# Head-pair sums moved from GpSimd to VectorE, T blocks loaded in place, results loaded among the last Strassen groups, LN begun later

## The chip, the cores and the metric

One NeuronCore of a Trainium2 chip. The metric is device microseconds of one execution of the whole layer; lower is better. The engines are called PE (TensorE; PEld are its weight loads), DVE (VectorE), ACT (ScalarE), POOL (GpSimd) and SP (SyncE, which issues nearly all transfers here).

## The reference

One layer of a hybrid backbone, in fp32: a modulated RMSNorm, one input projection to 56 column tiles of 128 beside q, k and v, three branches, and a gated merge.

```python
h, gate = modulate(x, c, ...)                    # 1024 tokens x 1024
z = h @ w_in                                     # 1024 x (11*512 + 3*1024)
kc, vc = na_kv(hc @ w_in[:, A_K:A_Z], ...)       # 256 context tokens
ya = neighbourhood_attention(q, k, v, kc, vc, rpb) * silu(z[A_Z:B_B])   # 8 heads of 64
yb = z[B_B:B_C] * dw_conv(z[B_C:B_V] * z[B_V:B_Z], w3) * silu(z[B_Z:C_GLU])
u  = dw_conv(a * sigmoid(g), w31) + b            # a, g: two 512-wide parts of z
yc = silu(layer_norm(u)) * silu(z[C_Z:GATES])
m  = ga * (ya @ w_out_a) + gb * (yb @ w_out_b) + gc * (yc @ w_out_c)    # ga, gb, gc: sigmoid of z[GATES:]
x  = x + gate * (m @ w_o)
```

## The kernel before, in words

Every fp32 product is made of three: each operand is split into a high part and the rest (`hi`, `lo`), and hi x hi, hi x lo and lo x hi are added in PSUM. The activations lie transposed: h is 16 tiles, `ha0` to `ha7` for the first 512 tokens and `hb0` to `hb7` for the others, each with its high part and its low part (128 x 2 x 512). `ACT` makes high parts by a cast, POOL or DVE the low ones by a subtraction (L90, L639).

Stages, in time: modulation and h (to about 100 us); four head pairs (`attend`, `qkv` of the next pair, `glu`), to about 540 us; a stage of Strassen groups, 565 to 943 us; three merges by `wout`, with the LN of the conformer branch among them, and the last projection by `wo`.

**Attention.** A head is 8 units. In a unit PE makes scores `sc` and `sl`, DVE finds their maximum and adds the bias (L544, L547; the bias comes from POOL), ACT takes exponentials, DVE adds sums, takes the reciprocal and scales (L551 to L554) in one of four buffers `pbuf`, PE transposes (`pp`, L564), ACT and DVE split the transposed blocks (`ph`, `plo`), PE multiplies with v (`py`), and DVE adds the halves into `ya` (L577; four times per head). PE needs something else to do in between: that is `glu` in the earlier pairs, and in the last one `plain(ZA + i)` and `plain(BZ + i)`, which make 16 halves (each 24 products into a bank `zaps`; `ps_m` has two banks) and evict them through a `flt` tile: sigmoid by ACT, product by DVE, store by SP.

**Sums of h.** `h_sums(j)` makes the four combinations of blocks of h that the Strassen stage multiplies with (T1 to T4) for k-block j: four sums of a high and a low part (`whole`, L598) and four differences (`less`, L603), each 128 x 512, and stores the results to `td` in DRAM. It runs on POOL, one j in each head pair. Its tiles come from `tmp`, a pool of six buffers that `flt` uses as well.

**T blocks.** Before the Strassen stage `load_t` loads `td` into `traw` tiles and splits them into T1 to T3; T4 goes into the place of `hb0` to `hb3`.

**Strassen stage.** Groups of products (banks `ga` to `ge`, `gd`) of `wz` with blocks of h and T1 to T4; among them the 31-tap convolution on DVE (`conv_step`, L690), and `a_result`, which multiplies attention by its gate on POOL and stores the split result. `last_two` are the last two groups. All results go to DRAM: `ysd` (ya, yb), `cvd` (convolution), `gd` (gates), `zcd`.

**Merges.** `merge(br, ys, beside)` goes over 8 blocks and two halves, 12 products `ops` each; POOL or DVE adds to `mt` (L980). `norm_steps` is the LN, cut into steps that `beside` calls: column sums (`col_sums`, PE), variances (L1041, POOL), `rstd` (diagonal tiles by DVE, PE product, L1051, L1052), then per half a DVE product, two ACT functions and two POOL products (L1064, L1066), and a split into `yc`.

**Order.** The program is written in this sequence, and a list scheduler with a timeline model of its own then sets each engine's row; `tc.issue_after(x)` holds what is inside it behind instruction x. Tiles of a pool are taken in the order of the text: a tile waits until the tile that had its buffer before is done with. Pools opened at a place that another pool had wait for that one.

Of the kernel before, what the change touches and what calls it, by code (L numbers as in the profile page):

```python
# [42 lines left out]
def tile_hybrid(ctx: ExitStack, tc, x, xT, cx, cond, crow, ng, w_ada, b_ada, wqkv, wz,  # L43
# [5 lines left out]
    hctx = ExitStack()  # L49
    hp_pool = hctx.enter_context(tc.tile_pool(name="hT", bufs=1))  # L50
# [79 lines left out]
    def qkv(hp, w=None, cts=None, first=(), psc=None, mid=None):  # L130
# [41 lines left out]
        def context():  # L172
            vc = [a1.tile([P, 2, P], F32R, tag=f"vc{h}", name="vc") for h in range(2)]
# [64 lines left out]
    A_t = cst.tile([P, KT, 2], F32, name="A_t")  # L238
    B_t = cst.tile([P, KT, 2], F32, name="B_t")
# [224 lines left out]
    with tc.tile_pool(name="at", bufs=1, reuse_waits="tile") as at, \  # L464
# [45 lines left out]
        def attend(hp):  # L510
            ya = at.tile([P, 16, 64], F32, tag="ya", name="ya", bufs=1)
            for h in range(2):
# [9 lines left out]
                for cb in range(4):  # L522
# [54 lines left out]
                    dve.tensor_tensor(out=ya[hs, :, cb * 16 : cb * 16 + 16],  # L577
# [16 lines left out]
        def h_sums(j):  # L594

            def whole(o, k):
                t = tmp("hsum")
                pool.tensor_tensor(out=t, in0=hlf[o][k][:, 0].bitcast(F32), in1=hlf[o][k][:, 1].bitcast(F32), op=ALU.add)  # L598
                return t

            def less(i, a, b):

                pool.tensor_tensor(out=b, in0=a, in1=b, op=ALU.subtract)  # L603
                nc.sync.dma_start(td[i][j], b)
# [9 lines left out]
        for hp in range(4):  # L614
# [12 lines left out]

    sctx = ExitStack()
# [34 lines left out]
    for i in (1, 0, 2):  # L663
        load_t(T[i], i)
    load_t(T4, 3)
# [99 lines left out]

    def last_two(cts, uses):
# [24 lines left out]
        for n in two:  # L791
# [4 lines left out]
            dve.tensor_tensor(out=x[n], in0=f, in1=x[n], op=ALU.add)  # L796
        s3 = [s_(n, raw[n][0], raw[n][2], ALU.subtract, "s3") for n in two]
# [7 lines left out]
        for n in two:  # L805
# [5 lines left out]
            uses[n][1](0, y[n])  # L811
        s4 = [s_(n, raw[n][1], s2[n], ALU.subtract, "s4") for n in two]
# [90 lines left out]

    for i in range(4):
        u = b_start(i)
        gate_pair()
        b_end(i, u)
    halves = [(i, b) for i in range(4) for b in range(2)]
    for i in range(5):
# [5 lines left out]
        for _ in range(1 + (i in (0, 2, 4))):  # L915
            a_result(*halves.pop(0))
# [7 lines left out]
    hctx.close()  # L924
# [277 lines left out]
```

## Time and profile before

| what | value |
|---|---|
| median of 3 runs | 1202.31 us (1201.91 to 1203.02) |
| profiled execution | 1200.33 us, span 1198.5 us |
| mean granted TensorE clock | 0.964 |
| PE busy | 1126.9 us (94%), 5566 matmuls |
| DVE busy | 850.8 us (71%) |
| POOL busy | 663.4 us (55%) |
| ACT busy | 560.8 us (47%) |
| moved by DMA | 167.87 MB, 139 GB/s of HBM |

A busy time is the time in which an engine had an instruction running; matmuls are pipelined, so PE at 100% of a stretch may still be slow where the granted clock (PEclk) is low. The span is the profiled program; the execution's own time is 1.83 us longer, and 2.0 us under the median. In rows of groups stand: line, engine, operation, output<-inputs, shapes and count, then busy us and mean ns, then idle us before them and what ended it.

### The profile page before, as it was taken

How to read it: one execution, taken by the hardware profiler on the slowest of the kernel's cores; microseconds unless marked ns; L12 is line 12 of the kernel's file. 1: busy time of each engine (PE TensorE's matmuls, PEld its weight loads, DVE VectorE, ACT ScalarE, POOL GpSimd, SP SyncE). 2: the span in 40 equal slices, each digit the busy share in tenths (PEclk: the TensorE clock that was granted, in tenths of full speed). 3: DMA queues.
4: the chain of work that ended last, by engine and by line, in shares of the span. 5: the costliest groups of instructions: out<-in, count | busy, mean ns of one | idle time of the engine just before them, and what ended most of it. 6: DMA issues, size and time to landing. Idle time of an engine off the chain costs nothing.

```text
span 1198.5 us, 16663 instructions
## 1 busy us (share of the span) xinstructions
PE 1126.9 (94%) x5566; PEld 961.0 (80%) x5566; DVE 850.8 (71%) x1495; ACT 560.8 (47%) x1167; POOL 663.4 (55%) x623
## 2 busy tenths in 40 slices
PE   5779699999999999998999999999999798999998
PEld 4678699899899788886788888887877476888887
DVE  7995768788877875657993897896993356679311
ACT  5575358557656688784333332324334335313110
POOL 6675845645745833310887677868888006851110
PEclk7789899999999999999899999999999798999999
DMA  9235242332322313117234434345653694662621
GB/s 354 106 136 180 72 126 84 104 108 85 111 64 77 118 63 121 56 42 236 93 102 142 124 105 149 101 154 173 190 192 132 242 406 153 205 241 88 237 80 53
DMA packets 88151, 167.87 MB, mean 140 GB/s; under 512 B 11008, under 2 KB 39424, under 8 KB 88064
## 3 DMA queue, kind: packets, MB, share of 16 engines
q1 hardware_dynamic: 83456, 164.70, 40.9%
q10 hardware_dynamic: 4608, 2.10, 0.6%
q8 instruction: 44, 0.72, 0.3%
q14 instruction: 43, 0.35, 0.1%
HBM read 120.62 MB, written 46.14 MB: 139 GB/s over the span
## 4 chain that ended last, share of the span: by engine, by line
PE 59%; DVE 17%; DMA 8%; POOL 7%; issue 4%; ACT 3%; SPq 1%; POOLq 0%; DVEq 0%; ACTq 0%
DVE cv L690 4%; PE ops L107 4%; PE ops L109 4%; PE ops L108 4%; PE pp L564 3%; PE zaps L108 3%; PE zaps L107 3%; PE zaps L109 3%; PE ps L109 3%; PE ps L107 3%; PE ps L108 3%; PE fin L109 2%; PE fin L107 2%; PE fin L108 2%; DMA wada<-in_w_ada 2%
## 5 line engine op out<-in xcount | busy, mean ns | idle before, releaser
L90 POOL TENSOR_TENSOR wl<-wr,wh 128x384 fp32r<-128x384 f32 (+2 forms) x93 | 89.6, 969 | 182.2 <-ACT wh L88 156.1
L690 DVE SCALAR_TENSOR_TENSOR cv<-upad,cf_t,cv 128x512 f32<-128x512 f32 x240 | 166.9, 747 | 0.2
L88 ACT CAST wh<-wr 128x384 fp32r<-128x384 f32 (+2 forms) x138 | 61.2, 456 | 113.5 <-DMA wr<-in_wout 46.9
L533 POOL TENSOR_TENSOR bias<-mka,vimg 128x288 f32<-128x288 bf16 (+1 forms) x64 | 59.5, 931 | 87.8 <-DVE mn L547 76.5
L639 POOL TENSOR_TENSOR wl<-s,wh 128x512 fp32r<-128x512 f32 x57 | 79.5, 1409 | 11.1 <-ACT wh L638 6.4
L638 ACT CAST wh<-s 128x512 fp32r<-128x512 f32 x76 | 46.1, 616 | 75.6 <-POOL s L642 64.1
L639 POOL TENSOR_TENSOR wl<-wr,wh 128x512 fp32r<-128x512 f32 x46 | 64.4, 1402 | 22.7 <-ACT wh L638 22.7
L569 DVE TENSOR_TENSOR plo<-pp,ph 128x512 fp32r<-128x512 f32 (+1 forms) x96 | 60.8, 640 | 8.5 <-ACT ph L567 8.0
L714 PE MATMUL ga<-ha,wh 128*128 128x512 f32 x152 | 60.6, 398 | 6.5 <-ACT wh L638 4.7
L564 PE MATMUL pp<-ident,pbuf 128*128 128x128 f32 x352 | 59.1, 273 | 1.6 <-DVE pbuf L553 1.3
L716 PE MATMUL ga<-ha,wl 128*128 128x512 f32 x152 | 60.3, 397 | 0.2 <-POOL wl L639 0.2
L715 PE MATMUL ga<-ha,wh 128*128 128x512 f32 x152 | 60.2, 396 | 0.0
L567 ACT CAST ph<-pp 128x512 fp32r<-128x512 f32 (+1 forms) x96 | 51.7, 547 | 16.8 <-PE pp L564 16.0
L549 ACT ACTIVATE pbuf<-sc,mn 128x256 f32<-128x256 f32 x64 | 30.4, 475 | 60.1 <-DVE mn L547 59.6
L1116 DVE SCALAR_TENSOR_TENSOR o<-fin,gate,xr 128x512 f32<-128x512 f32 x16 | 12.0, 751 | 59.7 <-PE fin L109 59.7
L551 DVE TENSOR_TENSOR mn<-mn 128x1 f32<-128x1 f32 x64 | 17.6, 275 | 47.0 <-ACT pbuf L550 46.7
L109 PE MATMUL fin<-mh,wl 128*128 128x512 f32 x128 | 49.8, 389 | 0.0
L108 PE MATMUL fin<-ml,wh 128*128 128x512 f32 x128 | 49.8, 389 | 0.0
L107 PE MATMUL fin<-mh,wh 128*128 128x512 f32 x128 | 49.7, 389 | 0.0
L564 PEld LDWEIGHTS pp<-ident,pbuf 128*128 128x128 f32 x352 | 42.7, 140 | 7.0 <-DVE pbuf L553 2.6
L90 DVE TENSOR_TENSOR wl<-wr,wh 128x384 fp32r<-128x384 f32 (+2 forms) x45 | 31.6, 705 | 13.9 <-ACT wh L88 13.9
L79 POOL TENSOR_TENSOR ssh<-ssh,half_neg 128x4 f32<-128x4 f32 (+1 forms) x40 | 39.4, 987 | 2.7
(382 smaller groups left out, 3970.3 us busy)
## 6 DMA issues: line engine op xcount, KB each, us to landing
wr<-in_wz SPq DMA_DIRECT2D x36, 512.0 KB, 3.9
gs<-gd SPq DMA_DIRECT2D x24, 512.0 KB, 5.2
wada<-in_w_ada SPq DMA_DIRECT2D x16, 512.0 KB, 8.7
wr<-in_wz SPq DMA_DIRECT2D x36, 192.0 KB, 2.5
cht<-chd SPq DMA_DIRECT2D x24, 256.0 KB, 3.1
gd<-gate SPq DMA_DIRECT2D x22, 256.0 KB, 3.1
vimg<-in_rpbs SPq DMA_DIRECT2D x16, 288.0 KB, 3.0
gd<-c SPq DMA_DIRECT2D x18, 256.0 KB, 3.1
```

The costliest lines, as they stand in the source:

```text
L88: act.copy(hi[:, :n], raw[:, :n])
L90: state["lo"] = lo_eng.tensor_tensor(out=lo[:, :n], in0=raw[:, :n], in1=hi[:, :n].bitcast(F32), op=ALU.subtract)
L107: pe.matmul(ps, ah, bh, start=i == 0, stop=False)
L108: pe.matmul(ps, ah, bl, start=False, stop=False)
L109: pe.matmul(ps, al, bh, start=False, stop=i == n - 1)
L564: pe.transpose(out=pp[:, c * 256 + hf * P : c * 256 + hf * P + P], in_=pts[hf][:, o : o + P], identity=ident)
L569: dve.tensor_tensor(out=plo[:, : m * 256], in0=pp[:, : m * 256], in1=ph[:, : m * 256].bitcast(F32), op=ALU.subtract)
L639: eng.tensor_tensor(out=lo, in0=src, in1=hi.bitcast(F32), op=ALU.subtract)
L690: dve.scalar_tensor_tensor(out=acc[b], in0=src, scalar=cf_t[:, i, j : j + 1], in1=acc[b], op0=ALU.mult, op1=ALU.add)
L714: pe.matmul(ps, wh, bh, start=first and j == 0, stop=False, skip_group_check=True)
L715: pe.matmul(ps, wh, bl, start=False, stop=False, skip_group_check=True)
L716: pe.matmul(ps, wl, bh, start=False, stop=last and j == 3, skip_group_check=True)
```

## The change

Five things change.

1. `h_sums` runs on DVE in place of POOL, and all four j stand in the last head pair, held behind the last `ya` addition of the third pair. In the text they still come ahead of `plain(ZA + i)`.
2. T1 to T3 get a pool of their own, `tp`, that stays open; `load_t` loads raw blocks straight into the low tile and splits in place. T2, T1, T3 are loaded ahead of the last two `plain` gates, T4 after the first `b_start`.
3. The pools of h and T stay open to the end. `mt`, `cv`, `ya`, `yb` take tiles of them, by a table `homes`, and `yb`, half of `ya` and `cv` are loaded inside `last_two`; the other loads are where a tile becomes free.
4. `a_result` is called once in the first loop's later steps and once per step of the second loop.
5. The LN's steps begin in the third block of the first merge, three per half; `rstd` is made by two products of 512 columns in place of eight of 128, with empty steps between its parts.

```diff
-    hctx = ExitStack()
-    hp_pool = hctx.enter_context(tc.tile_pool(name="hT", bufs=1))
+    hp_pool = ctx.enter_context(tc.tile_pool(name="hT", bufs=1, reuse_waits="tile"))
...
             def whole(o, k):
                 t = tmp("hsum")
-                pool.tensor_tensor(out=t, in0=hlf[o][k][:, 0].bitcast(F32), in1=hlf[o][k][:, 1].bitcast(F32), op=ALU.add)
+                dve.tensor_tensor(out=t, in0=hlf[o][k][:, 0].bitcast(F32), in1=hlf[o][k][:, 1].bitcast(F32), op=ALU.add)
...
-                pool.tensor_tensor(out=b, in0=a, in1=b, op=ALU.subtract)
+                dve.tensor_tensor(out=b, in0=a, in1=b, op=ALU.subtract)
                 nc.sync.dma_start(td[i][j], b)
...
-            h_sums(hp)
             if hp < 3:
                 glu(hp + 1)
+                last = state["ya"].ins
+        with tc.issue_after(last):
+            for j in range(4):
+                h_sums(j)
         for i in range(4):
             plain(ZA + i, zad[i])
...
-    T = [[pair(sp.tile([P, 2, 512], F32R, name=f"T{i}_{j}")) for j in range(4)] for i in (1, 2, 3)]
+    T = [[pair(tp.tile([P, 2, 512], F32R, tag=f"T{i}", name=f"T{i}", bufs=4)) for j in range(4)] for i in (1, 2, 3)]
...
-            t = s512("traw", "hs", 4)
-            nc.sync.dma_start(t, td[i][j])
-            split(*blocks[j], t, dve)
+            hi, lo = blocks[j]
+            nc.sync.dma_start(lo.bitcast(F32), td[i][j])
+            split(hi, lo, lo.bitcast(F32), dve)
+    for i in (1, 0, 2):
+        load_t(T[i], i)
     with tc.issue_after(state["py"].ins):
         for i in (6, 7):
             plain(GT + 2 * KT + i, gd[2 * KT + i], True)
-    for i in (1, 0, 2):
-        load_t(T[i], i)
-    load_t(T4, 3)
...
+    homes = {"mt": [f"ha{i}" for i in range(KT)], "cv": [f"hb{i}" for i in range(4)], "ya0": [f"hb{i}" for i in range(4, 8)],
+             "ya1": ["T3"], "yb": ["T1"] * 4 + ["T2"] * 4}
...
+        yb_s.extend(loaded_y(0, i, "yb") for i in range(4))
...
+        for i in range(4):
+            t = of("cv", "cvin", F32)
+            nc.sync.dma_start(t, cvd[i])
+            cv.append(t)
...
     for i in range(4):
         u = b_start(i)
+        if i == 0:
+            load_t(T4, 3)
         gate_pair()
+        if i:
+            a_result(*halves.pop(0))
         b_end(i, u)
...
-        for _ in range(1 + (i in (0, 2, 4))):
-            a_result(*halves.pop(0))
+        a_result(*halves.pop(0))
...
-    yb_s = [loaded_y(0, i, "yb") for i in range(4)]
...
-        cv.extend(loaded(cvd[i], "cvin", of("cv", "cvin", F32)) for i in range(4))
...
+        for b in range(2):
+            j = ltmp("diag")
+            for t in range(4):
+                dve.tensor_scalar(out=j[:, t * P : t * P + P], in0=ident, scalar1=var[:, b * 4 + t : b * 4 + t + 1], scalar2=None, op0=ALU.mult)
+            diags.append(j)
+        for _ in range(4):
+            yield
         for b in range(2):
             ps = ps_l.tile([P, 512], F32, tag="l", name="rstd")
-            for t in range(4):
-                j = ltmp("diag")
-                dve.tensor_scalar(out=j[:, :P], in0=ident, scalar1=var[:, b * 4 + t : b * 4 + t + 1], scalar2=None, op0=ALU.mult)
-                pe.matmul(ps[:, t * P : (t + 1) * P], ones, j[:, :P], start=True, stop=True)
+            pe.matmul(ps, ones, diags[b], start=True, stop=True)
             rstd.append(ps)
-            yield
+        yield
...
     def beside_b(dm, b):
         if (dm, b) == (4, 0):
             ya_s.extend(loaded_y(1, i, "ya") for i in range(4))
-        for _ in range(2):
+        for _ in range(3 if dm > 1 else 0):
             next(steps, None)
 
     def beside_a(dm, b):
         for _ in range(1 + b):
-            next(steps, None)
+            if next(steps, 0) == 0:
+                next(gsteps, None)
```

How this moves instructions is seen best at three places. First the sums. Before, POOL's row about the fourth head pair has the sums of the last j between the biases of attention and the low weight parts `wl`:

```order
L598 TENSOR_TENSOR hsum<-ha_178 128x512
L598 TENSOR_TENSOR hsum<-hb_625 128x512
L598 TENSOR_TENSOR hsum<-hb_724 128x512
L598 TENSOR_TENSOR hsum<-ha_182 128x512
L603 TENSOR_TENSOR hsum<-hsum 128x512
L533 TENSOR_TENSOR bias<-mka,vimg 128x288
L603 TENSOR_TENSOR hsum<-hsum 128x512
L90 TENSOR_TENSOR wl<-wr,wh 128x384
L603 TENSOR_TENSOR hsum<-hsum 128x512
```

After, DVE's row in the first head of the last pair, from the last `ya` addition of the third pair on, has them among the softmax:

```order
L580 TENSOR_TENSOR ya<-py,yl 64x16x16
L601 TENSOR_TENSOR hsum<-ha_175 128x512
L601 TENSOR_TENSOR hsum<-hb_463 128x512
L601 TENSOR_TENSOR hsum<-hb_682 128x512
L601 TENSOR_TENSOR hsum<-ha_179 128x512
L601 TENSOR_TENSOR hsum<-ha_176 128x512
L601 TENSOR_TENSOR hsum<-hb_517 128x512
L547 TENSOR_REDUCE mn<-sc 128x1
L554 TENSOR_TENSOR mn<-mn 128x1
L606 TENSOR_TENSOR hsum<-hsum 128x512
L572 TENSOR_TENSOR plo<-pp,ph 128x512 x2
L606 TENSOR_TENSOR hsum<-hsum 128x512
```

The sums are gone from POOL's row; in DVE's six come in one piece, and the others between two or three instructions of attention each.

Second, PE's filler in that head. Before, PE's row mixes the last pairs' attention with products of `plain` (`zaps`):

```order
L564 MATMUL pp<-ident,pbuf_1393 128x128 [waits PE_49]
L564 MATMUL pp<-ident,pbuf_1395 128x128
L564 MATMUL pp<-ident,pbuf_1393 128x128
L564 MATMUL pp<-ident,pbuf_1395 128x128 [waits DVE_49]
L107 MATMUL zaps<-hb_463,wh 128x512
L108 MATMUL zaps<-hb_463,wh 128x512
L109 MATMUL zaps<-hb_463,wl 128x512
L107 MATMUL zaps<-hb_517,wh 128x512
L108 MATMUL zaps<-hb_517,wh 128x512
L109 MATMUL zaps<-hb_517,wl 128x512
```

After, PE's row at the third half of `plain` (its first product reads `ha_175`, that is `ha0`) shows only attention for the rows ahead of it:

```order
L544 MATMUL sl<-ks,qd 128x288 [waits DVE_49]
L545 MATMUL sl<-ks,qlz_1386 128x288
L542 MATMUL sc<-kc,qd 128x256 [waits Activation_49]
L543 MATMUL sc<-kc,qlz_1386 128x256
L567 MATMUL pp<-ident,pbuf_1392 128x128 [waits DVE_49]
L567 MATMUL pp<-ident,pbuf_1390 128x128
L567 MATMUL pp<-ident,pbuf_1392 128x128 x2
L567 MATMUL pp<-ident,pbuf_1390 128x128
L567 MATMUL pp<-ident,pbuf_1392 128x128
L106 MATMUL zaps<-ha_175,wh 128x512 [waits DVE_49]
```

Between the last product of the second half and this one stand 107 products and transposes of attention and none of `zaps`; the wait on DVE is for the `flt` tile's product, which frees the bank.

Third, SP's row at the end of the Strassen stage, with results and the first output weights. Before, the weights go first and every result behind them:

```order
L837 DMA gd_153<-gate 128x512 [waits DMAHW5_49,Activation_49]
L86 DMA wr<-in_wout 128x384 [waits DMAHW6_49,PE_49,Pool_49]
L86 DMA wr<-in_wout 128x128 [waits DMAHW7_49]
L951 DMA cvin<-cvd_129 128x1024 [waits DMAHW0_49,PE_49]
L951 DMA cvin<-cvd_130 128x1024 [waits DMAHW1_49]
L837 DMA gd_153<-px 128x512 [waits DMAHW2_49,Activation_49]
L951 DMA cvin<-cvd_131 128x1024 [waits DMAHW3_49]
L951 DMA cvin<-cvd_132 128x1024 [waits DMAHW4_49,PE_49]
L86 DMA wr<-in_wout 128x384 [waits DMAHW5_49]
L86 DMA wr<-in_wout 128x128 [waits DMAHW6_49,Pool_49]
```

After, `yb`, four tiles of `ya` and `cvin` are already issued above these rows, and what is left of `ya` waits for PE and stands ahead of the weights:

```order
L789 DMA ya<-ysd_117 128x1024 [waits DMAHW3_49,PE_49]
L789 DMA ya<-ysd_118 128x1024 [waits DMAHW4_49,PE_49]
L871 DMA gd_151<-px 128x512 [waits DMAHW5_49,Activation_49]
L871 DMA gd_151<-gate 128x512 [waits DMAHW6_49,Activation_49]
L789 DMA ya<-ysd_119 128x1024 [waits DMAHW7_49,PE_49]
L871 DMA gd_153<-gate 128x512 [waits DMAHW0_49,Activation_49]
L85 DMA wr<-in_wout 128x384 [waits DMAHW1_49,Pool_49]
L85 DMA wr<-in_wout 128x128 [waits DMAHW2_49]
```

The results have moved from behind the first weights to ahead of them, with waits for products of the last groups.

More of the change, by code (lines that the diff above doesn't have):

```diff
@@ L172, in context @@
         def context():
+            if not state["vc"]:
+                a1.tile([P, 2 * L], F32R, tag="cht", name="cht", bufs=4)
+            state["vc"] = 1
             vc = [a1.tile([P, 2, P], F32R, tag=f"vc{h}", name="vc") for h in range(2)]
@@ L625, in tile_hybrid @@
     a1ctx.close()
+    tp = ctx.enter_context(tc.tile_pool(name="tp", bufs=1, reuse_waits="tile"))
     sctx = ExitStack()
@@ L764, in group, with of, loaded_y @@
         conv_step(3)
+    homes = {"mt": [f"ha{i}" for i in range(KT)], "cv": [f"hb{i}" for i in range(4)], "ya0": [f"hb{i}" for i in range(4, 8)],
+             "ya1": ["T3"], "yb": ["T1"] * 4 + ["T2"] * 4}
+    turn = dict.fromkeys(homes, 0)
+    def of(kind, name, dt=F32R):
+        tag = homes[kind][turn[kind] % len(homes[kind])]
+        turn[kind] += 1
+        if tag[0] == "T":
+            return tp.tile([P, S], dt, tag=tag, name=name, bufs=4)
+        return hp_pool.tile([P, S], dt, tag=tag, name=name)
+    def loaded_y(n, i, name):
+        out = []
+        for h in range(2):
+            t = of(("ya0", "ya1")[i // 2] if n else "yb", name)
+            nc.sync.dma_start(t.bitcast(F32), ysd[n][i][h])
+            out.append(t)
+        return out
+    yb_s, cv = [], []
     def last_two(cts, uses):
```

28 lines of the change are left out of this document (9 added, 19 removed).

## Prediction

> **What bounds the kernel.** I read the page first, then stretches of the span by engine, then TensorE's waits, then single groups.
>
> ```profile
> PE 1126.9 (94%) x5566; PEld 961.0 (80%) x5566; DVE 850.8 (71%) x1495; ACT 560.8 (47%) x1167; POOL 663.4 (55%) x623
> ```
>
> TensorE (PE; its weight loads PEld run beside it) is the bound: 94% busy, VectorE (DVE) next with 71%. So the change can only give back what TensorE loses at a few places, and costs what new holes it makes. The profiled execution took 1200.33 us (its span and what lies around it), 2.0 under the median of the runs, 1202.31: I sum against 1200.33 and add the 2.0 at the end. The stretches where it loses time (the stretch and its length, busy us and instructions of PE, PEld, DVE, ACT and POOL, granted clock, DMA share, GB/s):
>
> ```profile
> 130.00:155.00 25.00, 14.83 (x72) 13.78 (x71) 16.77 (x13) 6.38 (x14) 24.34 (x27) 0.80 0.14 47
> 140.00:145.00 5.00, 4.24 (x14) 4.27 (x15) 2.54 (x4) 0.42 (x1) 4.92 (x4) 0.50 0.00 0
> 405.00:415.00 10.00, 8.07 (x43) 6.19 (x42) 7.83 (x20) 4.19 (x13) 8.05 (x8) 1.00 0.53 159
> 535.00:550.00 15.00, 13.07 (x61) 10.72 (x60) 3.27 (x6) 4.75 (x9) 0.37 (x6) 0.89 0.39 133
> 565.00:580.00 15.00, 10.11 (x32) 7.37 (x31) 13.16 (x17) 7.61 (x15) 9.55 (x7) 0.77 0.53 188
> 570.00:575.00 5.00, 4.52 (x10) 3.16 (x11) 3.16 (x5) 2.21 (x5) 4.55 (x4) 0.50 0.69 274
> 940.00:970.00 30.00, 20.02 (x59) 12.87 (x58) 15.24 (x24) 15.02 (x28) 2.52 (x3) 0.72 0.93 350
> 985.00:1000.00 15.00, 10.73 (x40) 8.26 (x39) 7.70 (x23) 1.10 (x2) 2.82 (x3) 0.77 0.63 243
> 1000.00:1005.00 5.00, 5.00 (x23) 4.13 (x22) 3.96 (x6) 4.97 (x10) 3.76 (x4) 1.00 0.17 52
> ```
>
> A full stretch holds 23 matmuls in 5 us, 0.22 us each. Behind a gap the granted clock is 0.50, and 10 matmuls take 4.52 us: 2.3 us lost again. The losses are then: 130 to 155, 10.2 us idle and half of 4.24 us by the clock, 12.3; 405 to 415, 1.9; around 540 and 570, 1.9 + 4.9 + 2.3 = 9.1; 940 to 970, 30 less 59 x 0.22 = 17.0; 985 to 1000, 15 less 40 x 0.22 = 6.2. Their causes, from the waits of TensorE (us in all, times, longest):
>
> ```profile
> PE sl L541 <- DVE ks L505: 8.4, 1, 8.4
> PE sums L1006 <- ACT lnh L638: 7.7, 2, 7.2
> ...
> PE ga L714 <- ACT wh L638: 4.7, 1, 4.7
> PE rstd L1052 <- DVE diag L1051: 4.2, 1, 4.2
> PE gd L714 <- DVE c L720: 2.8, 3, 1.6
> ```
>
> **Sums of h off POOL: the gain.** The first wait (140.8 us) has its root in one add:
>
> ```profile
> L501 DVE TENSOR_TENSOR qlz<-qT,qd x8: 1218/1222/7415, 128.7 to 432.7; 64x1024 fp32r<-64x1024 f32 x8
> ```
> ```profile
> L603 POOL TENSOR_TENSOR hsum<-hsum x16: 1262/1296/1404, 143.0 to 416.3; 128x512 f32<-128x512 f32 x16
> ```
>
> The first add, at 128.7, took 7.4 us where the median is 1.2; POOL is busy 24.3 of the 25 us there, with eight sums of 1.3 us among them. Without the sums the add falls by up to 6.2 us and what POOL owes the queries comes sooner. I leave 3 of the 12.3 us (VectorE's copies stand in the way still): -9.3, between -6.2 and -12.3. At 405 to 415, the last sums: -2 (0 to -3).
>
> **The same sums on VectorE: the price.** All 32 but the last now stand in VectorE's row among the softmax of the seventh head, and `plain(ZA + i)`, TensorE's filler there, comes behind them in program order: its `flt` tiles share six buffers with the sums. The third half of `plain` waits for a `flt` multiply that stands behind 31 sums. Up to it TensorE has only that head's attention. VectorE's row from the last product of `plain`'s second half to that multiply holds 8 reduces, 7 score instructions with their accumulator reads, 8 adds, 7 reciprocals, 7 pairs of scalings, 10 `plo`, 4 `ya`, 1 `flt`, and 31 sums. The groups of VectorE's instructions from 451 to 500 us before, busy time, mean ns, idle time ahead:
>
> ```profile
> L569 DVE TENSOR_TENSOR plo<-pp,ph 128x512 fp32r<-128x512 f32 (+1 forms) x13 | 8.2, 642 | 1.1 <-ACT ph L567 1.1
> L547 DVE CUSTOM_DVE_ANT_0 pbuf<-sl,bias,mn 128x384 f32<-128x384 f32 (+1 forms) x9 | 5.1, 569 | 0.8 <-PE sl L542 0.4
> L591 DVE TENSOR_TENSOR flt<-zaps,flt 128x512 f32<-128x512 f32 x6 | 4.2, 692 | 5.7 <-ACT flt L589 5.7
> L553 DVE TENSOR_SCALAR pbuf<-pbuf,mn 128x384 f32<-128x384 f32 (+1 forms) x8 | 3.8, 480 | 0.3
> L554 DVE TENSOR_SCALAR pbuf<-pbuf,mn 128x256 f32<-128x256 f32 x8 | 3.5, 438 | 0.0
> L544 DVE TENSOR_REDUCE mn<-sc 128x1 f32<-128x256 f32 x8 | 3.3, 414 | 1.1 <-PE sc L540 1.1
> L577 DVE TENSOR_TENSOR ya<-py,yl 64x256 f32<-64x256 f32 x5 | 2.1, 412 | 0.0
> L552 DVE RECIPROCAL mn<-mn 128x1 f32<-128x1 f32 x8 | 1.3, 164 | 0.3
> L551 DVE TENSOR_TENSOR mn<-mn 128x1 f32<-128x1 f32 x8 | 1.3, 160 | 10.5 <-ACT pbuf L550 10.4
> L547 DVE DVE_READ_ACCUMULATOR2_ANT mn<- 128x1 f32 x9 | 0.8, 84 | 0.0
> ```
>
> These rows give 8 x 0.41 + 7 x 0.65 + 8 x 0.16 + 7 x 0.16 + 7 x 0.92 + 10 x 0.64 + 4 x 0.41 + 0.69 = 25.5 us. A sum on VectorE is not in the trace; the nearest add of two SBUF tiles of 128x512 is
>
> ```profile
> L639 DVE TENSOR_TENSOR T<-traw,T 128x512 fp32r<-128x512 f32 x8 | 5.2, 687 | 7.4 <-ACT T L638 7.4
> ```
>
> so 31 x 0.687 = 21.3, and 46.8 us in all. What TensorE does for such a piece, from 464 to 500 us before (all, then `zaps` alone, then the transposes `pp` alone):
>
> ```profile
> 464.00:500.00 36.00, 36.00 (x206) 31.26 (x205) 22.73 (x64) 29.49 (x58) 11.20 (x13) 1.00 0.23 77
> ```
> ```profile
> 464.00:500.00 36.00, 27.62 (x108) 18.95 (x107) 3.30 (x5) 2.39 (x4) 1.00 0.23 77
> ```
> ```profile
> 464.00:500.00 36.00, 6.43 (x40) 4.92 (x40) 5.83 (x10) 5.49 (x10) 1.00 0.23 77
> ```
>
> TensorE is full; `zaps` has 108 x 0.22 = 23.8 us of it, so attention with 40 transposes takes 12.2 us. The new piece has 39: 11.9. The hole is 46.8 - 11.9 = 34.9, less one of eight units (25.5 / 8, 3.1 us) that VectorE may be ahead: 31.8, and 2.3 for the clock behind it: +34. It is not given back: the work put off runs later on a TensorE that was full anyway. Lower end: VectorE as far ahead as its four `pbuf` buffers allow, three units more, +25. A sum that takes a tile again waits for its store to land, 2.4 us in the row below; six tiles in turn and attention between them give it that, and if not, what stands behind it on VectorE, the softmax, waits too. Upper end: the 10.4 us that it waited for ScalarE's exponentials (row L551) stay between the sums, +44.
>
> ```profile
> wr<-in_wz SPq DMA_DIRECT2D x36, 512.0 KB, 3.9
> ...
> td<-hsum SPq DMA_DIRECT2D x16, 256.0 KB, 2.4
> ```
>
> One rule speaks against the move in another way. Half of the eight adds of L501 took 1.22 us or less while POOL was busy 55% of the span, so I charge the sums nothing for POOL. The Trainium skill, "GPSIMD Engine Reference", Specs and Key points, says that GpSimd shares its SBUF interfaces with VectorE and that VectorE instructions with two SBUF inputs contend for them. The 7.4 us add agrees; the median of 1.22 doesn't show it. By the rows the sums cost 21.3 us, by the rule 30.9 (worked out as a rival below), and the total of +1.4 would be +11.0.
>
> **T blocks in place, at the end of attention.** Twelve loads and splits go ahead of TensorE's last filler (nine halves of `plain` stand behind the last attention product), so the splits are off the path. But the four loads of T4 wait until the last half has read `hb0` to `hb3`, and stand on SP ahead of the first Strassen weights: 12 products (2.6 us) are left when that half has read `hb3`; then the weights take 3.9 us to land (row wr<-in_wz above) and some 1.7 for the loads ahead and the cast: 3 us late instead of 4.7, plus 2.3 of clock. The gap at 540, attention's tail, goes. 9.1 becomes 5.3: -3.8 (0 to -9.1). `a_result`, one per step instead of two and one, takes something from the waits for VectorE's and POOL's products in the middle (row gd<-c, 2.8): -2 (+1 to -4).
>
> **Results loaded among the last groups.** `yb`, half of `ya` and `cv` are loaded up to 30 us before the last Strassen product. On SP the gates' stores stand behind these loads, which wait for products; the stores free tiles of which several are in turn, so I price that at nothing. The last two `ya` pairs and the first output weights still wait for products close to the end, so the weights go out as Strassen ends, as before:
>
> ```profile
> 942.69 0.87 SPq L86 DMA_DIRECT2D wr<-in_wout  x2
> ...
> 945.13 0.71 ACT L88 CAST wh<-wr 128x384 fp32r<-128x384 f32 x2 [0.78 <-DMA wr<-in_wout]
> ```
>
> 2.4 us to the cast, 0.7 for it and a little for `px`: the merge starts 3.4 us after Strassen, and the clock costs 2.3. Of 17.0 us 5.7 stay: -11.3 (-6 to -15).
>
> **LN later.** Its column sums now stand among the merge's products, and 40 products, 8.8 us, lie between the last of them and the wide `rstd` matmul. That is over twice the 4.2 us that `rstd` waited, so what it waits for is hidden. The loss at 985 to 1000 goes: -6.2 (-3 to -6.2). But POOL's part of LN now falls into one merge, whose weights and `mt` adds it has too:
>
> ```profile
> L980 POOL TENSOR_TENSOR mt<-mt,gs 128x512 f32<-128x512 f32 x10 | 13.5, 1351 | 9.1 <-DVE gs L979 4.7 <-PE ops L108 2.6 <-DMA wr<-in_wout 1.8
> L1066 POOL TENSOR_TENSOR zcin<-zcin,cvin 128x512 f32<-128x512 f32 x8 | 11.8, 1479 | 0.1
> L90 POOL TENSOR_TENSOR wl<-wr,wh 128x128 fp32r<-128x128 f32 (+1 forms) x13 | 11.8, 912 | 7.5 <-ACT wh L88 7.5
> ```
>
> 16 multiplies of about 1.4, 16 `mt` adds of 1.35 and 9 splits of 0.9 are 52 us beside a merge of 192 products, 42 us. The last `yc` may come late: +2 (0 to +10).
>
> **Sum.** +34 - 9.3 - 2 - 3.8 - 2 - 11.3 - 6.2 + 2 = +1.4; 1200.33 + 1.4 + 2.0 = 1204, own range 1198 to 1210. Less than 0.2%, 2.4 us, is about what a measurement of this kernel can't tell from no change.
>
> **Rivals.**
> - VectorE is four units ahead when the block begins. For it: it is busy only 22.7 of 36 us. Against: its next scores come from TensorE in the same row. 9.3 less: 1194. It decides if the third half starts under 30 us after the second ended.
> - Both transitions close wholly, 5.3 + 5.7 = 11 less: 1193. Against: the first weights stay behind end-of-stage loads.
> - The waits for exponentials stay: +10.4, 1214, slower. For: 10.4 us of them in 49 us before. Against: sums now fill them. It decides if VectorE is under 85% busy in the block.
> - Contention: as at 128.7, a sum stands still while POOL is at work. POOL works 11.2 of 36 us here (31%), so the sums take 21.3 / 0.69 = 30.9 us: +9.6, 1214, slower. It decides if the mean of a sum is 1 us. The skill's sentence on the shared interfaces is this case.
> - The change doesn't do what it says: the results are in place but products still begin 9 us after Strassen, behind late weights: half the gain, 1209.
> - POOL bounds the first merge: +8 more, 1212.
>
> **Chances.** The sum 0.33 (faster 0.06, same 0.10, slower 0.17); VectorE ahead 0.28 (0.25, 0.03, 0); transitions closed 0.10 (0.09, 0.01, 0); exponentials 0.11, contention 0.07, late results 0.07, POOL 0.04, all slower. Faster 0.40, same 0.14, slower 0.46. The range 1189 to 1216 takes in all of these and leaves out 2 in 10, for two of them together or a larger end of a term.
>
> **What would show it.** A dip of TensorE's busy share below 0.5 for some 40 us in the seventh head, with VectorE full and line L601's mean near 0.69; no add of 7 us at L504; the gap behind Strassen 3 to 4 us; no wait of the `rstd` matmul. The prediction is wrong if there is no such dip, or if the `zaps` products run on through it.

## The result: 1.5% slower, and where the time went

| kernel | median us | range | profiled execution, span, clock |
|---|---|---|---|
| before | 1202.11 | 1199.33 to 1203.02 (4 runs) | 1200.33, 1198.5, 0.964 |
| changed | 1219.76 | 1217.02 to 1221.06 (4 runs) | 1219.45, 1217.7, 0.954 |

The ratio is 1.0148, 95% interval 1.0124 to 1.0172: 17.7 us slower. The forecast was 1204, range 1189 to 1216: the place and the size of the new hole were right, two other terms were not. First the profile's page of the changed kernel:

```profile
span 1217.7 us, 16653 instructions
...
PE 1134.5 (93%) x5554; PEld 966.6 (79%) x5554; DVE 851.8 (70%) x1527; ACT 541.9 (45%) x1151; POOL 636.9 (52%) x591
```

TensorE still is the bound, at 93%; POOL has 27 us less to do, VectorE is where it was. The page does not show where the time went, so the program is cut at four places: the first `zaps` product, the first product into `ga`, the last one, and the first product of `fin` (the projection by `wo`). Each tile's view gives first and last start; these rows are of before, and then of the changed kernel.

```profile
L107 PE MATMUL zaps<-ha,wh x80: 387/390/632, 413.5 to 559.3; 128*128 128x512 f32 x80
...
L714 PE MATMUL ga<-ha,wh x152: 387/389/792, 570.3 to 940.8; 128*128 128x512 f32 x152
...
L716 PE MATMUL ga<-ha,wl x152: 388/389/796, 571.7 to 941.2; 128*128 128x512 f32 x152
...
L107 PE MATMUL fin<-mh,wh x128: 388/389/390, 1107.6 to 1193.9; 128*128 128x512 f32 x128
```

```profile
L106 PE MATMUL zaps<-ha,wh x80: 387/389/796, 402.9 to 580.0; 128*128 128x512 f32 x80
...
L721 PE MATMUL ga<-ha,wh x152: 389/389/796, 590.7 to 969.7; 128*128 128x512 f32 x152
...
L723 PE MATMUL ga<-ha,wl x152: 389/389/797, 592.5 to 970.2; 128*128 128x512 f32 x152
...
L106 PE MATMUL fin<-mh,wh x128: 389/389/389, 1126.8 to 1213.2; 128*128 128x512 f32 x128
```

From the first start to the first `zaps`, from there to `ga`, from first to last `ga`, and from there to `fin`, in us:

| stage | before | changed | difference | forecast |
|---|---|---|---|---|
| up to the first `zaps` | 413.5 | 402.9 | -10.6 | -11.3 |
| last head pairs, to the first `ga` | 156.8 | 187.8 | +31.0 | +34 - 3.8 = +30.2 |
| Strassen groups | 370.9 | 379.5 | +8.6 | -2 |
| merges and LN, to `fin` | 166.4 | 156.6 | -9.8 | -11.3 - 6.2 + 2 = -15.5 |
| sum | | | +19.2 | +1.4 |

The sum is the difference of the two spans (1217.7 - 1198.5). The last stage, `fin`, takes as long in both.

**The hole.** All engines in the stretch of the sums, and the sums alone (second row, from the sums' tile), in the changed kernel:

```profile
428.00:470.00 42.00, 24.85 (x94) 19.30 (x95) 39.29 (x90) 17.80 (x45) 12.60 (x10) 0.59 0.37 133
```

```profile
428.00:470.00 42.00, 20.38 (x31) 0.59 0.37 133
```

VectorE is 39.3 of 42 us busy, 20.4 of it with 31 sums; TensorE has 94 matmuls, where 36 us of the kernel before had 206. The granted clock is 0.59, so its 24.9 us of busy time hold some 15 us of work at the full clock (an estimate, 24.9 x 0.59). The products `zaps` stop at 420.6 us and come back at 467.7: 47 us, where the prediction had put this piece at 46.8. TensorE's busy share is 0.59 there, where the prediction had it below 0.5; the matmuls at the low clock count as busy for longer. VectorE's groups, and what it waited for:

```profile
L606 DVE TENSOR_TENSOR hsum<-hsum 128x512 f32<-128x512 f32 x15 | 10.4, 711 | 0.0
...
L601 DVE TENSOR_TENSOR hsum<-hb 128x512 f32<-128x512 f32 x8 | 5.3, 679 | 0.0
L601 DVE TENSOR_TENSOR hsum<-ha 128x512 f32<-128x512 f32 x8 | 5.3, 680 | 2.2 <-DMA td<-hsum 2.1
```

A sum takes 0.68 to 0.71 us in the mean of each group (0.687 was used). One wait for a store to land, 2.1 us, is the only long one; no wait for exponentials is left. The filler stands behind the sums on ScalarE too. The two halves of `plain` that TensorE had finished by 420.6 us get their sigmoid only here, though ScalarE was idle for 6.7, 4.0 and 3.5 us in between:

```profile
466.31 1.09 ACT L592 ACTIVATE flt<-zaps 128x512 f32<-128x512 f32 x2
```

**The Strassen stage.** TensorE is full but for two larger gaps and a few small ones. The largest:

```profile
875.00:880.00 5.00, 0.32 (x2) 0.00 (x0) 1.03 (x2) 0.90 (x2) 3.41 (x3) 0.93 0.40 148
880.00:885.00 5.00, 4.23 (x10) 3.36 (x11) 4.25 (x7) 3.33 (x7) 5.00 (x5) 0.50 0.30 115
```

Followed back in time order (start, duration, engine), from the matmul that waited:

```profile
865.64 0.86 SPq L702 DMA_DIRECT2D cvd<-cvo  x2
...
870.24 0.32 SPq L898 DMA_DIRECT2D yain<-yad  x1
870.65 1.15 SPq L738 DMA_DIRECT2D wr<-in_wz  x1
...
876.59 1.26 POOL L746 TENSOR_TENSOR s<-wr 128x512 f32<-128x512 f32 x1 [7.63 <-DMA wr<-in_wz]
877.80 1.26 POOL L900 TENSOR_TENSOR yain<-zain,yain 128x512 f32<-128x512 f32 x1
...
880.16 0.56 ACT L745 COPY p<-ga 128x512 f32<-128x512 f32 x1
...
880.77 0.79 PE L721 MATMUL ga<-ha,wh 128*128 128x512 f32 x1 [5.45 <-ACT p L745]
```

POOL stood 7.6 us without weights; the weights were issued at 870.65, right behind a load of `yain` on SP, and that load had waited for the convolution's stores of 865.64: `yain` and the convolution's results take turns in the four `ev` buffers. POOL then did `a_result`'s product, and ACT the copy `p` behind the cast of its result.

**The merges.** The first products wait 6.3 us, not 3.4, and another 4.6 us are lost where the third merge begins, on `ych` and `ycl`, the high and low part of the LN branch's result:

```profile
972.17 1.40 SPq L85 DMA_DIRECT2D wr<-in_wout  x3
...
977.61 1.19 ACT L87 CAST wh<-wr 128x384 fp32r<-128x384 f32 x3 [4.29 <-DMA wr<-in_wout]
978.18 0.80 PE L106 MATMUL ops<-yb,wh 128*128 128x512 f32 x1 [6.25 <-ACT wh L87]
...
1081.51 0.49 PE L106 MATMUL ops<-ych,wh 128*128 128x512 f32 x1 [1.99 <-ACT ych L645]
1084.59 0.79 PE L107 MATMUL ops<-ycl,wh 128*128 128x512 f32 x1 [2.58 <-DVE ycl L646]
```

The weights are issued as Strassen ends, as foreseen, but are cast 5.4 us after their issue (2.4 before). The DMA engines are full (share 1.02 to 1.03 from 945 to 965 us) with the results that now load there:

```profile
960.00:965.00 5.00, 5.00 (x24) 4.14 (x23) 3.19 (x6) 2.93 (x5) 0.00 (x0) 1.00 1.02 351
```

### The profile page after: what moved, and what is told of

It is laid out like the page before. It is cut to its first block, busy times and chain, and to the rows that moved or that the text cites. A ratio compares the mean times of both kernels' runs of the same rounds, so it can differ in the third digit from the quotient of the medians.

```text
span 1217.7 us, 16653 instructions
## 1 busy us (share of the span) xinstructions
PE 1134.5 (93%) x5554; PEld 966.6 (79%) x5554; DVE 851.8 (70%) x1527; ACT 541.9 (45%) x1151; POOL 636.9 (52%) x591
## 5 line engine op out<-in xcount | busy, mean ns | idle before, releaser
L536 POOL TENSOR_TENSOR bias<-mka,vimg 128x288 f32<-128x288 bf16 (+1 forms) x64 | 62.0, 969 | 135.4 <-DVE mn L550 120.3
L646 POOL TENSOR_TENSOR wl<-s,wh 128x512 fp32r<-128x512 f32 x57 | 82.0, 1452 | 2.9 <-ACT wh L645 2.2
L1143 DVE SCALAR_TENSOR_TENSOR o<-fin,gate,xr 128x512 f32<-128x512 f32 x16 | 12.0, 750 | 60.1 <-PE fin L108 60.1
L554 DVE TENSOR_TENSOR mn<-mn 128x1 f32<-128x1 f32 x64 | 15.7, 246 | 46.8 <-ACT pbuf L553 46.7
L721 PEld LDWEIGHTS ga<-ha,wh 128*128 128x128 f32 x152 | 29.6, 195 | 17.3 <-ACT p L745 6.5
L89 DVE TENSOR_TENSOR wl<-wr,wh 128x384 fp32r<-128x384 f32 (+2 forms) x45 | 27.5, 612 | 21.4 <-ACT wh L87 21.4
```

What stands on the lines that cost most here:

```text
L89: state["lo"] = lo_eng.tensor_tensor(out=lo[:, :n], in0=raw[:, :n], in1=hi[:, :n].bitcast(F32), op=ALU.subtract)
L536: pool.tensor_tensor(out=bv, in0=mv, in1=iv, op=ALU.subtract)
L646: eng.tensor_tensor(out=lo, in0=src, in1=hi.bitcast(F32), op=ALU.subtract)
L721: pe.matmul(ps, wh, bh, start=first and j == 0, stop=False, skip_group_check=True)
```

## The experiments

The stages of every kernel, worked out from first and last starts as above, in us; the ratio is to runs of the kernel before, taken beside them on the same chip.

| kernel | first `zaps` at | to `ga` | Strassen | to `fin` | median | ratio, interval |
|---|---|---|---|---|---|---|
| before | 413.5 | 156.8 | 370.9 | 166.4 | 1202.1 | |
| changed | 402.9 | 187.8 | 379.5 | 156.6 | 1219.8 | 1.0148 (1.0124 to 1.0172) |
| sums between the plain tiles | 402.3 | 160.5 | 379.9 | 155.6 | 1190.8 | 0.9902 (0.9873 to 0.9930) |
| sums on VectorE, one j a pair | 411.1 | 169.4 | 378.1 | 156.2 | 1207.5 | 1.0040 (1.0025 to 1.0055) |
| sums late, on POOL | 405.2 | 181.1 | 378.2 | 155.3 | 1213.1 | 1.0087 (1.0065 to 1.0109) |
| `a_result` as before | 402.9 | 188.7 | 371.8 | 157.7 | 1214.2 | 1.0089 (1.0068 to 1.0110) |
| six `ev` buffers | 401.8 | 189.5 | 376.1 | 156.0 | 1216.2 | 1.0117 (1.0090 to 1.0144) |
| `ya` loads later | 402.1 | 187.3 | 380.0 | 156.5 | 1218.1 | 1.0111 (1.0086 to 1.0136) |
| LN in block 0 | 402.1 | 188.4 | 378.1 | 149.5 | 1214.2 | 1.0074 (1.0050 to 1.0099) |
| no gate steps in the second merge | 401.8 | 188.1 | 380.3 | 155.2 | 1215.7 | 1.0088 (1.0056 to 1.0120) |
| between, `a_result` as before | 403.9 | 160.4 | 371.0 | 160.6 | 1186.2 | 0.9842 (0.9816 to 0.9868) |
| four edits | 402.4 | 160.2 | 370.4 | 152.4 | 1178.0 | 0.9799 (0.9773 to 0.9825) |
| between, `a_result` as before, LN in block 0 | 402.5 | 160.0 | 370.6 | 152.0 | 1177.9 | 0.9793 (0.9772 to 0.9815) |
| four edits, sums on POOL | 402.5 | 159.6 | 372.9 | 148.7 | 1176.8 | 0.9793 (0.9768 to 0.9818) |

### Sums between the plain tiles

```diff
-        with tc.issue_after(last):
-            for j in range(4):
-                h_sums(j)
         for i in range(4):
             plain(ZA + i, zad[i])
+            with tc.issue_after(last):
+                h_sums(i)
```

> The changed kernel with the sums of h still on VectorE and still behind the last ya of the third pair, but written one j behind each plain(ZA + i), so that plain's flt tiles come ahead of the sums in the six shared buffers. Theory (TensorE's filler waits for tiles and for its place behind the sums): the dip of TensorE between 425 and 470 us goes, some 25 to 31 us less than the changed kernel: 1189 to 1195 us. Rival (VectorE's 21 us of sums in that head are too much for it wherever they stand): the dip only moves, 1212 to 1220 us.

1190.8 us, 29 us less than the changed kernel and 1% faster than before, with the same sums on the same engine in the same head. TensorE there, in this kernel:

```profile
400.00:425.00 25.00, 25.00 (x139) 21.56 (x138) 19.66 (x45) 18.01 (x37) 9.38 (x10) 1.00 0.27 90
425.00:450.00 25.00, 20.85 (x111) 17.57 (x110) 19.17 (x45) 14.15 (x35) 8.51 (x10) 0.93 0.29 101
450.00:475.00 25.00, 24.98 (x132) 20.93 (x131) 21.80 (x50) 17.94 (x33) 6.73 (x8) 1.00 0.52 180
```

Of the hole 4.2 us are left (425 to 450). VectorE is now 60.6 of 75 us busy, so 21 us of sums fit beside the softmax as soon as `flt` tiles and TensorE's filler don't stand behind them. The first sigmoid of `flt` comes at 420 us here and the next two at 438. The cause of the hole is the place in the text. How the place acts, through the six buffers that sums and `flt` share or through the order that the scheduler makes of the text, is not told apart: no run gives the sums buffers of their own.

### Sums on VectorE in each pair

```diff
-        with tc.issue_after(last):
-            for j in range(4):
-                h_sums(j)
...
+            h_sums(hp)
```

> The changed kernel with the sums on VectorE, but one j in each head pair, at the places that they have in the kernel before. Theory (place, not engine): no dip, 1189 to 1197 us; the gain at 130 to 150 us stays, since POOL is free of the sums in both. Rival (VectorE can't carry the sums beside softmax): holes of 4 to 6 us in each pair, 1200 to 1212 us.

The call stands behind `qkv(hp + 1)`, as before the change. 1207.5 us: the theory's 1189 to 1197 is missed, and the time lies in the rival's range. But its holes of 4 to 6 us in each pair are not there: between the first pair and the first Strassen weights TensorE idles most at 340 to 360 us (2.8) and 530 to 550 (4.0), and not where the sums stand. The first scores come at 139.2 us (140.8 before, 133.9 in the changed kernel), so most of the gain at 130 to 150 us is gone though POOL is free of the sums. The add of L504 is short (at most 1.65 us), but VectorE itself is 19.0 of 25 us busy from 130 to 155, 13.3 in the changed kernel. So the gain came from taking the sums out of the first pair; taking them off POOL alone does not bring it. The 169.4 us from `zaps` to `ga` can't be compared with the other rows as they are: 29 matmuls of attention more lie behind this kernel's first `zaps`. Up to `ga` it takes 580.5 us, 10.2 more than before and 17.7 more than with the sums between the tiles; where these go is only in part shown.

### Sums late, on POOL

```diff
-                dve.tensor_tensor(out=t, in0=hlf[o][k][:, 0].bitcast(F32), in1=hlf[o][k][:, 1].bitcast(F32), op=ALU.add)
+                pool.tensor_tensor(out=t, in0=hlf[o][k][:, 0].bitcast(F32), in1=hlf[o][k][:, 1].bitcast(F32), op=ALU.add)
...
-                dve.tensor_tensor(out=b, in0=a, in1=b, op=ALU.subtract)
+                pool.tensor_tensor(out=b, in0=a, in1=b, op=ALU.subtract)
```

> The changed kernel with the sums at their new place, but on POOL. Theory (place, not engine): plain's flt tiles still come behind the sums; 31 sums of 1.3 us are 40 us on POOL, so the dip stays, 1215 to 1226 us. Rival (the dip is VectorE's time): it goes, 1189 to 1197 us.

1213.1 us, 2 under the theory's range, and far from the rival's. The hole stays with the sums on the other engine, 24 us against 31 (181.1 and 187.8 less 156.8). So most of it goes with the place, and some 7 us with the engine; on POOL the sums also begin earlier, at 392 us and not at 434. The first scores come at 133.8 us, as early as in the changed kernel.

### a_result as before the change

```diff
-        if i:
-            a_result(*halves.pop(0))
         b_end(i, u)
...
-        a_result(*halves.pop(0))
+        for _ in range(1 + (i in (0, 2, 4))):
+            a_result(*halves.pop(0))
```

> The changed kernel with a_result at the places of the kernel before (none in the first loop, 2, 1, 2, 1, 2 in the second). Theory (the Strassen stage is 8.6 us longer because a_result's loads and POOL products now stand with the b groups and behind the convolution's stores in every step): the stage falls to 371 us, 1210 to 1213 us. Rival (T in place and the convolution's earlier start make it longer): 1217 to 1221 us.

The Strassen stage falls from 379.5 to 371.8 us, against 370.9 before the change. Its extra 8.6 us are the places of `a_result`: 7.7 of them are shown by this run. The total lies 1 us above what was expected of the theory and 3 below the rival's.

### Six ev buffers

```diff
-        return sp.tile([P, 512], F32, tag="ev", name=name, bufs=4)
+        return sp.tile([P, 512], F32, tag="ev", name=name, bufs=6)
```

> The changed kernel with six ev buffers instead of four in the Strassen stage (convolution results, yain, zain and zb take turns in them). Theory (yain waits for the convolution's stores to land, and the group's weights stand behind it on SP): the stall of 5.5 us at 875 us goes with its clock loss, 5 to 7 us less, 1213 to 1215 us, with a_result where the change put it. Rival (POOL's two products per step beside the b groups are the cause, or the weights come late for POOL's splits): the stage stays at 378 to 380 us, 1218 to 1221 us.

Between the two. The stall at 875 us is gone; in its place stands, at 900 to 925 us, another of 4.0:

```profile
875.00:900.00 25.00, 25.00 (x112) 20.71 (x111) 25.00 (x40) 9.60 (x18) 20.38 (x16) 1.00 0.44 155
900.00:925.00 25.00, 20.99 (x90) 16.39 (x89) 20.88 (x31) 8.28 (x15) 19.48 (x16) 1.00 0.40 126
```

The stage takes 376.1 us. The queue on SP costs 3.4 us of the 8.6, as far as this shows it (in the kernels that change nothing in this stage it varies from 378.1 to 380.3 us); the rest goes with `a_result`'s other work per step. Most of TensorE's waiting among the groups is now for VectorE's sums `c`, which free the banks `gd` (4.2 us in the changed kernel, 0.7 with `a_result` as before the change):

```profile
PE gd L721 <- DVE c L727: 5.7, 4, 3.6
```

Which part of `a_result`'s work delays them isn't shown.

### The ya loads later

```diff
-            nc.sync.dma_start(raw[:, :n], src)
+            state["wdma"] = nc.sync.dma_start(raw[:, :n], src)
...
+            if (br, dm) == (1, 1):
+                state["hold"] = state["wdma"].ins
...
-            ya_s.extend(loaded_y(1, i, "ya") for i in range(4))
+            with tc.issue_after(state["hold"]):
+                ya_s.extend(loaded_y(1, i, "ya") for i in range(4))
```

> The changed kernel with the eight ya loads queued on SP behind the first weights of the second wout block. Theory (the first wout weights take 5.4 us to land instead of 2.4 because result loads fill the DMA engines, share 1.0 from 945 us on): the first weights land in 2.4 to 3.4 us, the merge starts 2 to 3 us sooner, 1216 to 1218 us. Rival (what counts is that the weights are issued only as Strassen ends): landing time and total stay, 1219 to 1221 us.

```profile
970.89 1.35 SPq L85 DMA_DIRECT2D wr<-in_wout  x3
...
973.74 1.20 ACT L87 CAST wh<-wr 128x384 fp32r<-128x384 f32 x3 [1.18 <-DMA wr<-in_wout]
974.30 0.80 PE L106 MATMUL ops<-yb,wh 128*128 128x512 f32 x1 [3.13 <-ACT wh L87]
```

The mechanism is as in the theory: 2.9 us from issue to cast instead of 5.4, and TensorE waits 3.1 us instead of 6.3. But from the last `ga` to `fin` it is 156.5 us against 156.6, and the median of 1218.1 lies between the theory's range and the rival's. The lead is gone by the end of the first merge: its last product comes 60.1 us behind the last `ga`, 60.3 in the changed kernel. In the ten microseconds shown TensorE does 33 matmuls, where a full stretch has 46 or more; among them are column sums of the LN, for which it waits 1.4 us in all:

```profile
1005.00:1010.00 5.00, 4.42 (x18) 2.93 (x16) 4.99 (x9) 2.94 (x6) 0.46 (x1) 1.00 0.85 316
1010.00:1015.00 5.00, 4.10 (x15) 2.65 (x15) 3.76 (x14) 3.44 (x8) 1.25 (x1) 1.00 0.44 126
```

The wait ahead of the third merge is as long as in the changed kernel, 4.7 us (there 2.0 for `ych` and 2.7 for `ycl`):

```profile
PE ops L106 <- ACT ych L645: 4.7, 1, 4.7
```

POOL, which makes `yc`, is busy without a break from 1045 to 1095 us in both. An earlier start of the first products bought nothing here.

### LN in block 0

```diff
-        for _ in range(3 if dm > 1 else 0):
+        for _ in range(3):
```

> The changed kernel with the LN's steps begun in block 0 of the first merge instead of block 2, three per half as before. Theory (POOL's part of LN falls into one merge and is late: TensorE idles 4.7 us at 1080 to 1085 and loses clock): the hole goes, 5 to 6 us less, 1213 to 1215 us. Rival (POOL's load in that merge is the same wherever LN begins): it stays, 1218 to 1221 us.

From the last `ga` to `fin` 149.5 us, 7.1 less than the changed kernel, and no wait for `ych` or `ycl` is left; 1.2 of the 7.1 lie in the wait for the first weights, which varies as much without this edit (5.0 to 6.4 us), and `fin` itself takes 0.8 longer:

```profile
PE ops L106 <- ACT wh L87: 5.1, 1, 5.1
...
PE ops L108 <- POOL wl L89: 1.1, 1, 1.1
```

The median of 1214.2 is in the theory's range. It was the delay of two blocks that made POOL late.

### No gate steps in the second merge

```diff
-            if next(steps, 0) == 0:
-                next(gsteps, None)
+            next(steps, None)
```

> The changed kernel without the gate vector's steps in the second merge (they run in the third). Theory (POOL's adds take 2.25 us instead of 1.3 from 1062 to 1084 because VectorE's reduces of two 128x1024 SBUF tiles run beside them): POOL's adds fall to 1.3 us, POOL saves some 9 us and the hole at 1080 shrinks to 0 or 1 us, 1213 to 1216 us. Rival (POOL simply has 52 us of work in 42): the hole stays, 1218 to 1221 us.

The waits for `ych` and `ycl` fall from 4.7 us to 3.3; in kernels with the same LN they are 3.5 to 4.8. In the changed kernel POOL's adds are stretched while VectorE reduces `gw` (first two rows); here, without the reduces, they are not, until these begin at 1076.8 (last two):

```profile
1069.40 2.27 POOL L1002 TENSOR_TENSOR mt<-mt,gs 128x512 f32<-128x512 f32 x1
...
1070.46 2.30 DVE L1108 CUSTOM_DVE_ANT_0 gw<-gw,crs 128x1024 f32<-128x1024 f32 x1
```

```profile
1069.92 1.28 POOL L1002 TENSOR_TENSOR mt<-mt,gs 128x512 f32<-128x512 f32 x1
...
1080.00 2.28 POOL L1092 TENSOR_TENSOR zcin<-zcin,cvin 128x512 f32<-128x512 f32 x1
```

From the last `ga` to `fin` it is 1.4 us less, but kernels with the same merges differ by as much (155.3 to 157.7). The contention is there; that it makes a part of the hole is not shown clear of that spread. The expected 0 to 1 us of hole is not reached, and the reduces still run beside the last of POOL's products. The median (1215.7) lies where the theory had it, but the stage doesn't show it, so how much the contention costs in all is left undecided.

### Between, and a_result as before

Both edits together.

> Two edits together on the changed kernel: sums written one j behind each plain(ZA + i), and a_result at the places of the kernel before. Theory (two separate stages, so the gains add): 1190.8 less 5.6 to 7.7, 1183 to 1185 us. Rival (with the sums spread, the Strassen stage begins otherwise and the a_result gain is lost): 1189 to 1192 us.

1186.2 us, 1 above the theory's range, at 1204.6 of the kernel before beside it. The two stages take 160.4 and 371.0 us, so both gains are there in full; 4 us are lost in the merges (160.6 against 156.6), where the first weights are now cast 6.7 us after their issue and TensorE waits 9.3 us for them, not 6.3:

```profile
939.02 2.13 SPq L85 DMA_DIRECT2D wr<-in_wout  x3
945.72 1.28 ACT L87 CAST wh<-wr 128x384 fp32r<-128x384 f32 x3 [7.30 <-DMA wr<-in_wout]
```

### Four edits, and three

The edits of the later `ya` loads and of LN in block 0 on top of the last kernel; then the same with the sums on POOL; then, with the sums on VectorE, without the later `ya` loads.

> Four edits on the changed kernel: sums one j behind each plain(ZA + i), a_result as before the change, ya loads behind the first weights of the second wout block, LN begun in block 0. Theory: the kernel with the first two (1186.2) loses its 9.3 us wait for the first wout weights down to 3 to 4, and the POOL hole in the second merge (some 5 us): 1174 to 1179 us. Rival (ya later only moves the loss to the second merge, as it did alone): 1180 to 1184 us.

> The same four edits with the sums on POOL, between the plain tiles. Theory (in that stretch POOL has room and VectorE is the one that softmax waits for): the remaining 4 us of idle TensorE at 425 to 450 go, 2 to 5 us less than with the sums on VectorE, 1171 to 1176 us. Rival (POOL's sums delay the bias and the low weight parts): 0 to 4 us more, 1176 to 1182 us.

> The four edits with the sums on VectorE, without the later ya loads. Theory (the later ya loads count as soon as POOL's hole in the second merge is gone): the first weights land 5 to 7 us after their issue again and nothing wins it back, so the stage from the last ga to fin takes 155 to 157 us instead of 152.4, 1181 to 1184 us. Rival (their gain is lost in the merges all the same): 152 to 153 us, 1177 to 1179 us.

1178.0, 1176.8 and 1177.9 us: 2.0 to 2.1% faster than before the change. The first lies in its theory's range, the other two in the rivals'. On which engine the sums run, once they stand between the plain tiles, makes no difference that can be told (intervals 0.9773 to 0.9825 and 0.9768 to 0.9818). On POOL 3.2 of the 4.2 us at 425 to 450 do go, as expected, but the stage is only 0.6 us shorter, the Strassen groups take 2.5 us longer and the merges 3.7 less; why is not shown. The later `ya` loads make no difference either, and here my theory fell. Without them TensorE waits 8.7 us for the first output weights, with them 3.1, and yet the stage takes 152.0 and 152.4 us. Where the 5.6 us went shows in the second merge, first without, then with the later loads:

```profile
1000.00:1020.00 20.00, 20.00 (x90) 16.57 (x89) 19.79 (x24) 10.72 (x19) 19.82 (x12) 1.00 0.73 235
1020.00:1040.00 20.00, 20.00 (x90) 16.54 (x89) 14.04 (x16) 5.76 (x11) 20.00 (x16) 1.00 0.77 243
```

```profile
1000.00:1020.00 20.00, 20.00 (x90) 16.54 (x90) 20.00 (x22) 10.10 (x17) 20.00 (x13) 1.00 0.70 237
1020.00:1040.00 20.00, 17.08 (x74) 13.53 (x73) 12.24 (x16) 3.38 (x8) 20.00 (x16) 1.00 0.76 254
```

POOL is full in both. TensorE, started earlier, loses 2.9 us there and 1.3 at 960 to 980 us (18.67 of 20 busy, 20.0 in the other), all of it waits for low weight parts `wl`, 2.9 us from POOL and 1.3 from VectorE. Where the rest of the 5.6 goes is not shown. The two last edits take 8.2 us off the stage (160.6 to 152.4), and LN in block 0 alone as much (to 152.0).

## Why the prediction was wrong, by its steps

- **The price of the sums on VectorE: right.** +30.2 us forecast for the stage with the T blocks, +31.0 measured. A sum took 0.69 us, VectorE was 94% busy in the hole, TensorE had attention alone there, and the piece without `zaps` was 47.0 us long (46.8 forecast). The rivals on that place fall: VectorE was not four units ahead (that asked for under 30 us), the exponentials cost no wait, and the sums were not slowed by POOL (0.68 to 0.71 us in the mean with POOL 30% busy). The nearness of 30.2 to 31.0 is in part luck. With the sums between the tiles the same stage, less 4.2 us idle and some 1.5 lost by the clock (20.85 x 0.07), is 154.8 us. So by this estimate the T blocks gave some 2 us and not 3.8, and the hole cost 33 to 35 (kernels with this stage unchanged take 187.3 to 189.5), near the 34 of the sum. TensorE still waits 4.4 us for the first Strassen weights (4.7 before, 3 forecast).
- **Sums off POOL: right in size, the cause half told.** -10.6 against -11.3 us; the add of L501 (L504 in the changed kernel) is at most 1.93 us now (7.4 before), as forecast. But taking the sums off POOL is not enough. With the sums on VectorE in the first pair the add was short too, and nearly all of the gain was gone (first scores at 139.2 us); with the sums late on POOL it was there (133.8). What helps is that the sums leave that place.
- **`a_result`: the step that failed first.** "-2 (+1 to -4)" was 8.6 us of loss, outside its own ends; with `a_result` back, the stage is 371.8 us. I let it save waits in the middle and did not count the loads that it issues: `yain` stands on SP ahead of the weights and waits for a buffer that the convolution's stores hold. By the run with six buffers that queue is 3.4 us of the 8.6. The rest goes with the same step, by a way that stays open. This term is 10.6 of the 17.8 us that the sum missed.
- **Results among the last groups: the mechanism right, a term missing.** The wait ahead of the first merge was 6.3 us where I had 3.4. I took the landing time of the weights, 2.4 us, from a row ahead of which the DMA engines were about a third busy (share 0.27 to 0.42 from 930 to 942.6 us); the moved loads fill them (share 1.02). The rival "results in place, late weights" priced this with half the gain. Moving four megabytes of `ya` behind the weights won 3.1 us at the start of the first merge, and they were lost again by its end.
- **LN later: right in place, mis-sized.** No wait of `rstd` is left, as forecast. The late `yc` was +2 (0 to +10) and is 4.7 us of waits and some clock; starting in block 0 took 7.1 us off the stage. With the bullet above this is nearly all of the 5.7 us by which the last stages gained less than forecast.
- **The likeliest sum** was thus short by 17.8: 0.7 and 0.8 in the first two stages, 10.6 and 5.7 in the others. The range ended at 1216 because I let one case at a time go wrong; two did, in different stages.

## What to carry to other kernels

Moving work to an engine with idle time pays only if nothing that another engine lives on stands behind it: look at who takes the next tile of the same pool, and write filler ahead of the work that it hides. For each moved step list its loads too, with what they wait for on the issuing queue and what is queued behind; and take a landing time from a stretch in which the queue is as full as it will be. When a gain disappears, look for what the freed engine waits for next: the weights that landed 2.5 us sooner brought nothing, as TensorE then waited for the LN's column sums in one kernel and for low weight parts, most of them POOL's, in another.

## What the runs showed of the hardware

- VectorE and POOL slow each other down on two-input work from SBUF, in some pairs of instructions and not in others. In the second merge POOL's 128x512 add took 1.28 us without VectorE's reduce of two 128x1024 tiles and 2.27 beside it, and the reduce between 1.45 and 2.3 us. In the hole, where the prediction weighed this, it was POOL that lost. A `bias` took 4.19 us beside VectorE's sums (the row below), where the same stage of the kernel before has 0.73 to 0.93:

```profile
447.50 4.19 POOL L536 TENSOR_TENSOR bias<-mka,vimg 128x288 f32<-128x288 bf16 x1 [5.28 <-DVE mn L550]
```

  All of VectorE's sums but one took 0.67 to 0.69 us there; that one, beside another `bias`, took 1.22. The Trainium skill, "GPSIMD Engine Reference", Specifications, names contention of POOL with VectorE instructions that have two SBUF inputs. The rows agree that it exists; the prediction's rival had the loss on the wrong engine.
- TensorE's granted clock stayed at 0.50 for some 25 us in the hole though TensorE was not idle; five-microsecond stretches of the changed kernel:

```profile
440.00:445.00 5.00, 4.24 (x16) 3.21 (x15) 5.00 (x14) 1.80 (x6) 1.18 (x1) 0.50 0.65 202
445.00:450.00 5.00, 2.52 (x11) 2.43 (x11) 5.00 (x13) 1.89 (x6) 2.50 (x1) 0.50 0.35 132
...
460.00:465.00 5.00, 2.00 (x8) 1.52 (x7) 5.00 (x13) 1.45 (x5) 1.04 (x1) 0.50 0.42 159
```

At 40 to 85% busy the clock did not come back in these 25 us. What the slow matmuls cost there isn't separated; VectorE, 94% busy, was the bound.
